# Rotary halves of the queries at rows 0 and 64: the turned copy read from the other rows, not multiplied, and a new order table for the middle

## The chip, the cores and the metric

The kernel runs on one core of one Trainium2 chip, in one launch. The metric is the device time in microseconds; before the change three runs gave 1440.78, 1445.82 and 1445.23 us, a median of 1445.23.

## What is computed

One layer of a hybrid trunk for 1056 tokens: 1024 of a new prompt and 32 of a running stream with 512 cached positions. Three mixers (latent attention with 6 heads, an S5 state-space model, RWKV-7 with 6 heads) read one input projection and meet in one output projection; a layer norm, a squared-ReLU MLP and a second layer norm follow. The change touches the attention's queries:

```python
cos, sin = rope_tables(pos)
q = (rms_norm(q_lat, prm['q_norm_g']) @ prm['w_qb']).reshape(b, t, MLA_HEADS, NOPE_DIM + ROPE_DIM)
q_nope = q[..., :NOPE_DIM]
q_rope = apply_rope(q[..., NOPE_DIM:], cos, sin)
...
x1, x2 = jnp.split(xf, 2, axis=-1)
return (xf * c + jnp.concatenate([-x2, x1], -1) * s).astype(x.dtype)
```

Each head has 64 columns without rotation (nope) and 32 with it (rope). A rotated row is the row times a cosine, plus the row of the other half of the 32 (the turned copy) times a sine whose sign depends on the half.

## The kernel before

The work stands in this order: the input projection to about 241 us of the profiled execution, then stage_q (241 to 262), the middle (262 to about 676) in which attention, S5 and RWKV are interleaved, the output projection with the first layer norm, and the MLP from some 780 us on. The program is written as stages; a scheduler with a timeline model of its own then sets the order of instructions on each engine, within what the code ties down. Tokens lie along the free axis, 1056 columns, cut in three blocks of 384, 384 and 288.

**stage_q** (L1175 to L1228) turns the normalized query latent qn (256 x 1056) into the queries. Its function product (L1184 to L1192) makes 128 rows of output: for each of the three blocks two matmuls with a weight of 128 columns (k is the half of the 256), named scq, and an eviction by ScalarE. Six products are made: qrope (the 32 rotary rows of heads 0 to 3), qturn (the same rows with their halves exchanged, multiplied from a second copy of the weight whose columns are exchanged), qropeb (for heads 4 and 5 rows and turned rows together, 64 and 64), and three qnope, two heads each (L1202). wqa and wqr are the weights: wqr is loaded with 8 DMAs on ScalarE's queue (L1199), wqa with two on SP's. ropec and ropes hold cosines and signed sines, repeated per head (four loads each, L1210 on SP's queue, L1211 on ScalarE's). VectorE does the rotation with six operations: L1215 to L1217 on 128 rows for heads 0 to 3, and L1222 to L1224 on 64 rows for heads 4 and 5, where L1222 reads qropeb's rows 64 to 127 and writes rows 0 to 63. The results go to q_d in DRAM: four stores of 32 rows (L1220) and two qnope stores on SP's queue, the rest on GpSimd's. attn_q (L1231) reads a head's 96 rows back.

**Behind stage_q on SP's queue** stand loads of the cached keys (ct, kt; the rows in which the new rotary keys kr arrive, L1107, are cleared around by two VectorE memsets, L1115 and L1116), the first head's q, the stores zt_d and xt_d of RWKV operands (zt is a VectorE copy, L778, after a loop of L774 and L775), and the loads zb and zc of them (L791, L792), which the pti matmuls (L802) of the RWKV inversion read. Of the kr rows ScalarE makes the rounded kh, VectorE the remainder kl (split3, L49 and L50); the attention's score matmuls sc and st (three each, L63, L65, L67) need both.

**The middle** (L1363) pulls one step at a time from four streams, as the letters of the string PLAN say: F is the front of a head's attention (sc, and the maximum mx on VectorE), O its back (st, the exponential ptk on ScalarE, the product with the values av, L1289), S is the RWKV scan (names that begin with pr, such as pra, prt, prw, and pti), X is S5 (s5e L643, s5y, s5l). Each step is tied behind the TensorE instruction of the step before it, so PLAN sets TensorE's order to a large part. S5 reads em by SP's queue (L632); after its last block it stores z_d, reads it back turned as zt (8 DMAs on SP's queue and 8 on GpSimd's, L690), and applies a gelu on ScalarE (L697) with a table load before and behind it. An out-projection (acc<-wo,m) starts in the middle's last part as filler; its last input is mg_d, the store of the last head's ot, which comes back as mraw and is split to mh and ml. z is the first layer norm (L1540 to L1543), which TensorE turns (pt, L1562).

Of the kernel before, what the change touches and what calls it, by code (L numbers as in the profile page):

```python
# [8 lines left out]
F32 = mybir.dt.float32  # L9
F32R = mybir.dt.float32r  # L10
AF = mybir.ActivationFunctionType
ALU = mybir.AluOpType
# [5 lines left out]
P = 128  # L18
T = 1056
# [707 lines left out]
def hsl(i):  # L727
    return slice(64 * i, 64 * i + 64)
# [446 lines left out]
def stage_q(g):  # L1175


    nc = g.nc
    i = 0

    def f(name):
        return g.p1.tile([P, T], F32, tag="f", name=name, bufs=5)

    def product(out, w):  # L1184
        nonlocal i
        for s, n in BLK:
            pool, tag = ((g.pfs, "fs"), (g.pt, "pt"))[i % 2]
            i += 1
            ps = pool.tile([P, 512], F32, tag=tag, name="scq")[:, :n]
            for k in range(2):  # L1190
                nc.tensor.matmul(out=ps, lhsT=w[:, k], rhs=g.qn[:, k, s:s + n], start=k == 0, stop=k == 1)  # L1191
            nc.scalar.activation(out=out[:, s:s + n], in_=ps, func=AF.Copy)  # L1192

    wa = f("wqa")[:, :768].rearrange("p (k h c) -> p k h c", k=2, c=64)
    wr = f("wqr")[:, :768].rearrange("p (k j x) -> p k j x", k=2, x=P)
    for k in range(2):
        nc.sync.dma_start(out=wa[:, k], in_=g.a["w_qb"][:, k, :, 0:64])
        for h, n, c, j, x in ((0, 4, 64, 0, 0), (0, 4, 96, 1, 0), (4, 2, 64, 2, 0), (4, 2, 96, 2, 64)):
            nc.scalar.dma_start(out=wr[:, k, j, x:x + 32 * n].rearrange("p (h c) -> p h c", c=32), in_=g.a["w_qb"][:, k, h:h + n, c:c + 32])  # L1199
    qs_ = g.xp.tile([P, KD, T], F32, tag="xl", name="qnope")  # L1200

    def nope(p):  # L1202
        q = qs_[:, KD - 3 + p]
        product(q, wa[:, :, 2 * p:2 * p + 2].rearrange("p k h c -> p k (h c)"))
        for h in range(2):
            (nc.gpsimd if p else nc.sync).dma_start(out=g.q_d[2 * p + h, 0:64], in_=q[hsl(h)])

    cs, sn = f("ropec"), f("ropes")
    for h in range(4):
        nc.sync.dma_start(out=cs[32 * h:32 * h + 32], in_=g.a["rope"][0:32])  # L1210
        nc.scalar.dma_start(out=sn[32 * h:32 * h + 32], in_=g.a["rope"][32:64])  # L1211
    qa, qs, qb, qt = (g.p1.tile([P, 1152], F32, tag="kk", name=x, bufs=3)[:, :T] for x in ("qrope", "qturn", "qropeb", "qturnb"))
    product(qa, wr[:, :, 0])
    product(qs, wr[:, :, 1])
    nc.vector.tensor_tensor(out=qa, in0=qa, in1=cs, op=ALU.mult)  # L1215
    nc.vector.tensor_tensor(out=qs, in0=qs, in1=sn, op=ALU.mult)
    nc.vector.tensor_tensor(out=qa, in0=qa, in1=qs, op=ALU.add)  # L1217
    nope(0)
    for h in range(4):
        nc.sync.dma_start(out=g.q_d[h, 64:96], in_=qa[32 * h:32 * h + 32])  # L1220
    product(qb, wr[:, :, 2])
    nc.vector.tensor_tensor(out=qt[0:64], in0=qb[64:128], in1=sn[64:128], op=ALU.mult)  # L1222
    nc.vector.tensor_tensor(out=qb[0:64], in0=qb[0:64], in1=cs[0:64], op=ALU.mult)
    nc.vector.tensor_tensor(out=qb[0:64], in0=qb[0:64], in1=qt[0:64], op=ALU.add)  # L1224
    nope(1)
    nope(2)
    for h in range(2):
        nc.gpsimd.dma_start(out=g.q_d[4 + h, 64:96], in_=qb[32 * h:32 * h + 32])  # L1228


def attn_q(g, h):  # L1231
# [131 lines left out]
def middle(g, scan):  # L1363
# [36 lines left out]


PLAN = (
    "FFFFFFFFSFSFFSFFFFFFSFFFFFFFFFFFSFOOSOFSOOOSFOOOSSOSOOSFSOFOFOOOOOOSXOSOOFSFOSXOOOOFOOOSFFSSSOSSOOXF"
    "FXFOSFOFOSOSXFFFOOFSOSSOSXOOSFSFSOOFSOFXXOSOFOFOOOOSOFSSOFOXOOXFSOOOFOFOOSOXSSSOOSOFSOFXSFSFOOFFSSFX"
    "FFFSFFFSXOOSFOOSOFOOSOOXFSSOOSXFOSOOSOOSFXOOOOFOOXOSFSSOOFSSOXOSOOOOOFOSXOFFSOXSFSFFSFFSFFSOOXSOSFFX"
    "SSFOOSOOOXOSOOOFSOOOOOFSOFOOSOOXSOFSSOXOFOOSFXXFOXOSSOOFSOSFXOOOOSSFOFSXFFFSFFFFSFFFSXFFFSFFSOXOOSSO"
    "OFSOXOSFFOSOSOXOFSOOFSOXFOSOSXOSFOOOSOOOOOFSSOSXSFOOOOSFOXFOXOSOSFOFOSSSFFSFFOOSSOOOOOOOOOOSOOOOSOFS"
    "SOSSOOOOSSOSOOOOOOOOOOOOOO"
)


# [803 lines left out]
def tile_trunk(ctx, tc, a, o):  # L2215
# [31 lines left out]
    with ExitStack() as s1:  # L2247
# [47 lines left out]
        nc.sync.dma_start(out=g.o["sh_s"], in_=sho[10:20])  # L2295
        stage_u(g)
        stage_q(g)
        s2.close()
    g.pt = None
# [144 lines left out]
```

## Time and profile before

| | us |
|---|---|
| median of three runs (lowest, highest) | 1445.23 (1440.78, 1445.82) |
| the profiled execution's own time | 1446.23 |
| its span, first to last instruction | 1444.5 |
| TensorE busy in the span | 1378.9 |
| mean granted TensorE clock, of full speed | 0.976 |
| stage_q's 72 scq matmul records | 241.0 to 262.2 |

A line of the timeline gives start, duration, engine, line, operation, out<-in, shapes, a count, and in brackets how long the engine had been idle and what ended that. A wait row gives the waiting engine and line, what released it, then the sum in us, the number of times and the longest. A row of the windows gives for a stretch its length, the busy time of each engine with the number of instructions, the granted clock (1.00 is full), the DMA share and GB/s. In a row of one tile, three numbers with strokes are the shortest, median and longest duration in ns. An fp32 matmul shows as two records.

### The profile page before, as it was taken

To read this page: it belongs to the slowest core of one execution; us is meant where nothing else is said; L and a number is where in the kernel's file an instruction comes from. 1 tells how busy PE (TensorE), PEld (TensorE's weight loads), DVE (VectorE), ACT (ScalarE), POOL (GpSimd) and SP (SyncE) were. 2 spreads that over 40 slices of the span, in tenths; PEclk is the share of its full clock that TensorE was granted. 3 is DMA by queue.
4 is the path that set the end of the run, shared out by engine and by line. 5 is a ranking of instruction groups with operands and counts; after the bars stand their busy time and mean duration, and the time that the engine had idled before them with its cause. 6 is when DMAs were issued, how large, how long until landed. Compare 5 with 4: busy or idle time off the path is not lost.

```text
span 1444.5 us, 28201 instructions
## 1 busy us (share of the span) xinstructions
PE 1378.9 (95%) x11532; PEld 1238.2 (86%) x11532; DVE 981.1 (68%) x1793; ACT 656.6 (45%) x1143; POOL 114.9 (8%) x228
## 2 busy tenths in 40 slices
PE   9999999789999879899998999999999999999996
PEld 9989898576777657667688999999999999999996
DVE  7666979655666755664769876666655786665577
ACT  6645543435454545552326344444444443434332
POOL 1411100400000100200200000000000000000022
PEclk9999999799999999899999999999999999999998
DMA  5433553941343420244434444344429695354232
GB/s 204 148 124 136 173 158 92 235 84 51 92 108 89 97 55 27 80 128 135 121 106 152 156 166 150 122 161 147 145 107 392 226 323 164 96 180 129 64 103 77
DMA packets 149431, 198.59 MB, mean 137 GB/s; under 512 B 53393, under 2 KB 97093, under 8 KB 148793
## 3 DMA queue, kind: packets, MB, share of 16 engines
q1 hardware_dynamic: 128492, 176.19, 38.5%
q10 hardware_dynamic: 20072, 18.50, 4.2%
q0 software_dynamic: 736, 2.09, 0.6%
q8 instruction: 90, 1.47, 0.4%
q14 instruction: 41, 0.33, 0.1%
HBM read 129.42 MB, written 67.28 MB: 136 GB/s over the span
## 4 chain that ended last, share of the span: by engine, by line
PE 81%; DVE 9%; ACT 4%; DMA 2%; issue 2%; SPq 1%; POOL 0%; ACTq 0%; DVEq 0%; POOLq 0%
PE acc L63 20%; PE acc L67 20%; PE acc L65 20%; PE av L1289 3%; PE scq L1191 1%; DMA wo<-in_w_out 1%; DVE mx L1260 1%; PE st L63 1%; PE sc L63 1%; PE st L65 1%; PE st L67 1%; PE scv L1169 1%; PE prw L896 1%; DVE xo L50 1%; PE pti L802 1%
## 5 line engine op out<-in xcount | busy, mean ns | idle before, releaser
L63 PE MATMUL acc<-xo,wo 128*128 128x272 f32 (+1 forms) x896 | 254.7, 285 | 2.8 <-ACT wo L49 2.8
L67 PE MATMUL acc<-xo,wo 128*128 128x256 f32 (+1 forms) x896 | 253.6, 285 | 1.6 <-DVE wo L50 1.6
L65 PE MATMUL acc<-xo,wo 128*128 128x272 f32 (+1 forms) x896 | 253.7, 284 | 0.0
L67 PE MATMUL acc<-hop,wo 128*128 128x272 f32 (+1 forms) x896 | 194.4, 284 | 0.0
L63 PEld LDWEIGHTS acc<-xo,wo 128*128 128x128 f32 x896 | 168.8, 189 | 3.0 <-ACT wo L49 3.0
L67 PEld LDWEIGHTS acc<-xo,wo 128*128 128x128 f32 x896 | 168.4, 189 | 2.0 <-DVE wo L50 2.0
L65 PEld LDWEIGHTS acc<-xo,wo 128*128 128x128 f32 x896 | 169.3, 189 | 0.0
L63 PE MATMUL acc<-hop,wo 128*128 128x256 f32 (+1 forms) x768 | 159.1, 285 | 0.0
L65 PE MATMUL acc<-hop,wo 128*128 128x272 f32 (+1 forms) x768 | 158.3, 283 | 0.0
L67 PEld LDWEIGHTS acc<-hop,wo 128*128 128x128 f32 x896 | 142.4, 188 | 0.0
L63 PE MATMUL acc<-xh,wmhi 128*128 128x384 f32 (+3 forms) x384 | 127.2, 332 | 2.1 <-ACT ckv L204 1.8
L65 PE MATMUL acc<-xl,wmhi 128*128 128x384 f32 (+3 forms) x384 | 128.1, 334 | 0.7 <-DVE xl L50 0.6
L67 PE MATMUL acc<-xh,wmlo 128*128 128x384 f32 (+3 forms) x384 | 127.1, 332 | 0.0
L65 PEld LDWEIGHTS acc<-hop,wo 128*128 128x128 f32 x768 | 119.6, 189 | 0.0
L63 PEld LDWEIGHTS acc<-hop,wo 128*128 128x128 f32 x768 | 118.7, 188 | 0.0
L49 ACT ACTIVATE wo<-wr 128x512 fp32r<-128x512 f32 (+1 forms) x64 | 47.0, 739 | 117.9 <-PE acc L67 68.0
L1289 PE MATMUL av<-ptk,vo 128*128 128x512 f32 (+5 forms) x204 | 74.5, 450 | 10.3 <-ACT ptk L1314 9.0
L50 DVE TENSOR_TENSOR hop<-hraw,hop 128x1056 fp32r<-128x1056 f32 (+3 forms) x58 | 70.4, 1214 | 13.8 <-ACT hop L49 13.7
L50 DVE TENSOR_TENSOR wo<-wr,wo 128x512 fp32r<-128x512 f32 (+1 forms) x64 | 52.3, 822 | 40.3 <-ACT wo L49 40.3
L63 PEld LDWEIGHTS acc<-xh,wmhi 128*128 128x128 f32 (+1 forms) x384 | 71.7, 187 | 5.2 <-ACT ckv L204 1.9
L65 PEld LDWEIGHTS acc<-xl,wmhi 128*128 128x128 f32 (+1 forms) x384 | 71.6, 187 | 4.4 <-DVE xl L50 1.3
L67 PEld LDWEIGHTS acc<-xh,wmlo 128*128 128x128 f32 (+1 forms) x384 | 71.7, 187 | 3.5 <-issue 1.6
(558 smaller groups left out, 2973.2 us busy)
## 6 DMA issues: line engine op xcount, KB each, us to landing
hraw<-h_d SPq DMA_DIRECT2D x48, 528.0 KB
wr<-in_w_up SPq DMA_DIRECT2D x35, 512.0 KB
h_d<-hx SPq DMA_DIRECT2D x16, 792.0 KB
h_d<-ht SPq DMA_DIRECT2D x16, 792.0 KB
wd<-in_w_dn SPq DMA_DIRECT2D x16, 512.0 KB
wr<-in_w_dn SPq DMA_DIRECT2D x16, 512.0 KB
ld<-rw SPq DMA_DIRECT2D x24, 320.0 KB
wmraw<-in_w_m SPq DMA_DIRECT2D x12, 512.0 KB
```

What stands on the lines that cost most here:

```text
L49: nc.scalar.activation(out=hi, in_=ps, func=AF.Copy)
L50: (lo_eng or nc.vector).tensor_tensor(out=lo, in0=ps, in1=hi.bitcast(F32), op=ALU.subtract)
L63: nc.tensor.matmul(out=outs[i], lhsT=lh, rhs=rhs[i][0], start=start, stop=False, **kw)
L65: nc.tensor.matmul(out=outs[i], lhsT=lh, rhs=rhs[i][1], start=False, stop=False, **kw)
L67: nc.tensor.matmul(out=outs[i], lhsT=ll, rhs=rhs[i][0], start=False, stop=stop, **kw)
L802: nc.tensor.matmul(out=ps[64 * c:64 * c + 32, t], lhsT=l[rows, t], rhs=z[rows, t], start=True, stop=True)
L896: nc.tensor.matmul(out=pw[hsl(c), p - p0, h], lhsT=g.xt[p][hsl(c), t, h], rhs=r[hsl(c), p, K_A:K_NV + 1:K_NV, h], start=True, stop=True)
L1169: nc.tensor.matmul(out=ps[:n, j], lhsT=c, rhs=g.wkv[:, 1, p * P:p * P + P], start=True, stop=True)
L1191: nc.tensor.matmul(out=ps, lhsT=w[:, k], rhs=g.qn[:, k, s:s + n], start=k == 0, stop=k == 1)
L1260: nc.vector.tensor_reduce(out=mx[:n, t, b // 512:b // 512 + 1], in_=ps[:n, :w], axis=AX.X, op=ALU.max)
L1289: nc.tensor.matmul(out=po[:, c:n], lhsT=vo[:w, kt].rearrange("p a x -> p (a x)")[:, 64 * i:64 * i + P], rhs=pt[:w, c:n], start=kt == tiles ...
```

## The change

The rotary columns of the weight are laid out anew: first halves (16 rows of each head) from row 0, second halves from row 64. Then the turned copy of a row is the row 64 further on, or back, and qturn's product goes; wr shrinks from three groups to two. Heads 4 and 5 take 96 rows: 0 to 31 first halves, 32 to 63 a filler (the first halves again), 64 to 95 second halves. product takes outputs of fewer than 128 rows.

VectorE's rotation becomes nine operations. For heads 0 to 3: two products on 64 rows that read one half of q and write the other half of a temporary (qropet), one product with the cosine and one sum on 128 rows. For heads 4 and 5: two products on 32 rows, one on 96, two sums on 32. A half of a head is 16 rows, so the loads and stores are cut finer: wqr 10 loads instead of 8 (ScalarE's queue), ropes 8 loads of 16 rows on SP's queue instead of 4 of 32 on ScalarE's, qrope 8 stores of 16 rows on SP's queue instead of 4, qropeb 4 on GpSimd's instead of 2. The rotation is a generator (turn), whose stores are issued after nope(0).

```diff
-                nc.tensor.matmul(out=ps, lhsT=w[:, k], rhs=g.qn[:, k, s:s + n], start=k == 0, stop=k == 1)
-            nc.scalar.activation(out=out[:, s:s + n], in_=ps, func=AF.Copy)
+                nc.tensor.matmul(out=ps[:out.shape[0]], lhsT=w[:, k], rhs=g.qn[:, k, s:s + n], start=k == 0, stop=k == 1)
+            nc.scalar.activation(out=out[:, s:s + n], in_=ps[:out.shape[0]], func=AF.Copy)
...
-        for h, n, c, j, x in ((0, 4, 64, 0, 0), (0, 4, 96, 1, 0), (4, 2, 64, 2, 0), (4, 2, 96, 2, 64)):
-            nc.scalar.dma_start(out=wr[:, k, j, x:x + 32 * n].rearrange("p (h c) -> p h c", c=32), in_=g.a["w_qb"][:, k, h:h + n, c:c + 32])
+        for h, n, c, j, x in ((0, 4, 64, 0, 0), (0, 4, 80, 0, 64), (4, 2, 64, 1, 0), (4, 2, 64, 1, 32), (4, 2, 80, 1, 64)):
+            nc.scalar.dma_start(out=wr[:, k, j, x:x + 16 * n].rearrange("p (h c) -> p h c", c=16), in_=g.a["w_qb"][:, k, h:h + n, c:c + 16])
...
-        nc.scalar.dma_start(out=sn[32 * h:32 * h + 32], in_=g.a["rope"][32:64])
-    qa, qs, qb, qt = (g.p1.tile([P, 1152], F32, tag="kk", name=x, bufs=3)[:, :T] for x in ("qrope", "qturn", "qropeb", "qturnb"))
-    product(qa, wr[:, :, 0])
-    product(qs, wr[:, :, 1])
-    nc.vector.tensor_tensor(out=qa, in0=qa, in1=cs, op=ALU.mult)
-    nc.vector.tensor_tensor(out=qs, in0=qs, in1=sn, op=ALU.mult)
-    nc.vector.tensor_tensor(out=qa, in0=qa, in1=qs, op=ALU.add)
+        for a in range(2):
+            nc.sync.dma_start(out=sn[64 * a + 16 * h:64 * a + 16 * h + 16], in_=g.a["rope"][48 - 16 * a:64 - 16 * a])
+
+    def turn(name, m, w, heads):
+
+        q, t = (g.p1.tile([P, 1152], F32, tag="kk", name=x, bufs=3)[:, :T] for x in (name, name + "t"))
+        product(q[0:m], w)
+        r = m - 64
+        for a in range(2):
+            nc.vector.tensor_tensor(out=t[64 * a:64 * a + r], in0=q[64 - 64 * a:64 - 64 * a + r], in1=sn[64 - 64 * a:64 - 64 * a + r], op=ALU.mult)
+        nc.vector.tensor_tensor(out=q[0:m], in0=q[0:m], in1=cs[0:m], op=ALU.mult)
+        for x in ((slice(0, P),) if r == 64 else (slice(0, r), slice(64, m))):
+            nc.vector.tensor_tensor(out=q[x], in0=q[x], in1=t[x], op=ALU.add)
+        yield
+        for j, h in enumerate(heads):
+            for a in range(2):
+                (nc.sync if h < 4 else nc.gpsimd).dma_start(out=g.q_d[h, 64 + 16 * a:80 + 16 * a], in_=q[64 * a + 16 * j:64 * a + 16 * j + 16])
+
+    ta, tb = turn("qrope", P, wr[:, :, 0], range(4)), turn("qropeb", 96, wr[:, :, 1, 0:96], (4, 5))
+    next(ta)
     nope(0)
-    for h in range(4):
-        nc.sync.dma_start(out=g.q_d[h, 64:96], in_=qa[32 * h:32 * h + 32])
...
+    next(ta, None)
+    next(tb)
     nope(1)
     nope(2)
-    for h in range(2):
-        nc.gpsimd.dma_start(out=g.q_d[4 + h, 64:96], in_=qb[32 * h:32 * h + 32])
+    next(tb, None)
```

PLAN gets a new string of the same kind; its first line as an example:

```diff
-    "FFFFFFFFSFSFFSFFFFFFSFFFFFFFFFFFSFOOSOFSOOOSFOOOSSOSOOSFSOFOFOOOOOOSXOSOOFSFOSXOOOOFOOOSFFSSSOSSOOXF"
+    "FFFFFFFFSFSFFFFFFFSFSFFFFFFFFFFFSFOOSOFSOOOSFOOOSSOSOOSFSOFOFOOOOOOOOSSXOFSOFSXOFOOOFOOOSFSSSOSSOOXF"
```

What this makes of the order, in three places. First SP's queue behind stage_q, before and then after (q_d holds the queries, ct, kt and kr are keys):

```order
L1220 DMA q_d<-qrope 32x1056 x2
L1206 DMA q_d<-qnope 64x1056 x2
L1220 DMA q_d<-qrope 32x1056 x2
L1088 DMA ct<-in_ckv 128x4x128
L1094 DMA kt<-in_kr 128x4x32
L1107 DMA kr<-kr_d 32x1056
```

And after:

```order
L1206 DMA q_d<-qnope 64x1056 x2
L1227 DMA q_d<-qrope 16x1056 x8
L1088 DMA ct<-in_ckv 128x4x128
L1094 DMA kt<-in_kr 128x4x32
L1107 DMA kr<-kr_d 32x1056
```

The qnope stores stand first, and eight short qrope stores in place of four stand between them and the key loads. The rest of the queue (q, zt_d, xt_d, zb, zc) keeps its order.

Second, TensorE at the first s5e of S5, in the middle's first quarter; the piece of the difference, lines with a minus are of before:

```order
-L896 MATMUL prw<-r,xt 64x128 x12
-L643 MATMUL s5e<-ut,em 128x133 x2
-L1289 MATMUL av<-ptk,vo 128x32
-L847 MATMUL pra<-ld 64x128 x12
+L1297 MATMUL av<-ptk,vo 128x32
 L63 MATMUL st<-qh,kh 128x512
 L65 MATMUL st<-ql,kh 128x512
 L67 MATMUL st<-qh,kl 128x512
-L1289 MATMUL av<-ptk,vo 128x32
+L896 MATMUL prw<-r,xt 64x128 x12
+L847 MATMUL pra<-ld 64x128 x12
+L643 MATMUL s5e<-ut,em 128x133 x2
```

s5e moved behind one group of st (128x512) and behind pra.

Third, TensorE at the S5 output, where av waits for an exponential that ScalarE makes after the gelu; before, with the waiting av as the last row:

```order
L847 MATMUL pra<-ld 64x128 x12
L63 MATMUL st<-qh,kh 128x512
L65 MATMUL st<-ql,kh 128x512
L67 MATMUL st<-qh,kl 128x512
L1132 MATMUL sck<-ckv,wkv 128x32
L854 MATMUL prt<-ident,ld 128x128 x8
L1289 MATMUL av<-ptk,vo 128x512
L63 MATMUL st<-qh,kh 128x512
L65 MATMUL st<-ql,kh 128x512
L67 MATMUL st<-qh,kl 128x512
L1289 MATMUL av<-ptk,vo 128x512
```

And after, again up to the av whose exponential follows the gelu on ScalarE:

```order
L1297 MATMUL av<-ptk,vo 128x512
L847 MATMUL pra<-ld 64x128 x12
L63 MATMUL st<-qh,kh 128x512
L65 MATMUL st<-ql,kh 128x512
L67 MATMUL st<-qh,kl 128x512
L854 MATMUL prt<-ident,ld 128x128 x8
L1297 MATMUL av<-ptk,vo 128x512
L63 MATMUL st<-qh,kh 128x512
L65 MATMUL st<-ql,kh 128x512
L67 MATMUL st<-qh,kl 128x512
L854 MATMUL prt<-ident,ld 128x128 x4
L1297 MATMUL av<-ptk,vo 128x512
```

Ahead of these rows one more group of st (128x512) stands since the change, and one exponential more is made before the gelu; so one st, one av and four prt more lie between the loads of zt and the waiting av. Elsewhere in the middle steps are exchanged in many places; the last av of the middle has 86 and not 105 of the output projection's matmuls ahead of it. Outside stage_q the TensorE instructions are the same ones.

More of the change, by code (lines that the diff above doesn't have):

```diff
@@ L1190, in product @@
             for k in range(2):
-                nc.tensor.matmul(out=ps, lhsT=w[:, k], rhs=g.qn[:, k, s:s + n], start=k == 0, stop=k == 1)
-            nc.scalar.activation(out=out[:, s:s + n], in_=ps, func=AF.Copy)
+                nc.tensor.matmul(out=ps[:out.shape[0]], lhsT=w[:, k], rhs=g.qn[:, k, s:s + n], start=k == 0, stop=k == 1)
+            nc.scalar.activation(out=out[:, s:s + n], in_=ps[:out.shape[0]], func=AF.Copy)
     wa = f("wqa")[:, :768].rearrange("p (k h c) -> p k h c", k=2, c=64)
-    wr = f("wqr")[:, :768].rearrange("p (k j x) -> p k j x", k=2, x=P)
+    wr = f("wqr")[:, :512].rearrange("p (k j x) -> p k j x", k=2, x=P)
     for k in range(2):
         nc.sync.dma_start(out=wa[:, k], in_=g.a["w_qb"][:, k, :, 0:64])
-        for h, n, c, j, x in ((0, 4, 64, 0, 0), (0, 4, 96, 1, 0), (4, 2, 64, 2, 0), (4, 2, 96, 2, 64)):
-            nc.scalar.dma_start(out=wr[:, k, j, x:x + 32 * n].rearrange("p (h c) -> p h c", c=32), in_=g.a["w_qb"][:, k, h:h + n, c:c + 32])
+        for h, n, c, j, x in ((0, 4, 64, 0, 0), (0, 4, 80, 0, 64), (4, 2, 64, 1, 0), (4, 2, 64, 1, 32), (4, 2, 80, 1, 64)):
+            nc.scalar.dma_start(out=wr[:, k, j, x:x + 16 * n].rearrange("p (h c) -> p h c", c=16), in_=g.a["w_qb"][:, k, h:h + n, c:c + 16])
     qs_ = g.xp.tile([P, KD, T], F32, tag="xl", name="qnope")
@@ L1210, in stage_q @@
         nc.sync.dma_start(out=cs[32 * h:32 * h + 32], in_=g.a["rope"][0:32])
-        nc.scalar.dma_start(out=sn[32 * h:32 * h + 32], in_=g.a["rope"][32:64])
-    qa, qs, qb, qt = (g.p1.tile([P, 1152], F32, tag="kk", name=x, bufs=3)[:, :T] for x in ("qrope", "qturn", "qropeb", "qturnb"))
-    product(qa, wr[:, :, 0])
-    product(qs, wr[:, :, 1])
-    nc.vector.tensor_tensor(out=qa, in0=qa, in1=cs, op=ALU.mult)
-    nc.vector.tensor_tensor(out=qs, in0=qs, in1=sn, op=ALU.mult)
-    nc.vector.tensor_tensor(out=qa, in0=qa, in1=qs, op=ALU.add)
-    nope(0)
-    for h in range(4):
[L1220 to L1224, printed above, removed]
+        for a in range(2):
[15 more added lines that the diff above has]
+    next(ta)
+    nope(0)
+    next(ta, None)
+    next(tb)
     nope(1)
     nope(2)
-    for h in range(2):
-        nc.gpsimd.dma_start(out=g.q_d[4 + h, 64:96], in_=qb[32 * h:32 * h + 32])
+    next(tb, None)
 def attn_q(g, h):
@@ L1402 @@
 PLAN = (
-    "FFFFFFFFSFSFFSFFFFFFSFFFFFFFFFFFSFOOSOFSOOOSFOOOSSOSOOSFSOFOFOOOOOOSXOSOOFSFOSXOOOOFOOOSFFSSSOSSOOXF"
[L1404 to L1408, printed above, removed]
+    "FFFFFFFFSFSFFFFFFFSFSFFFFFFFFFFFSFOOSOFSOOOSFOOOSSOSOOSFSOFOFOOOOOOOOSSXOFSOFSXOFOOOFOOOSFSSSOSSOOXF"
+    "FXFOSFOFOSOSXFFFFOOSOSSOSOXOSFSFOSFSOOFXOXOSFOFOOOOSOFFSSOXOFOOXOOSOFOFOOOXSOOSSSOFSSOFXSFSFOOFFSSFX"
+    "FFFSFFFSOXOSFOOSOFOOXFSOOSSSXOOFSSOOOOSOFXOOOOFOOXOSFSSOOOFSSOXOSOOOOFOSXOFFFFSOXFFSFSSFFSSOOXSOSFFO"
+    "XSSFOSOOOXOSOOOFSOOOOOFSOFOOOOOSXFOSOSSXFOOFXSXFXOOOSOSFOSSFXOOOOSSFOXFSFFFSFFFFSFFFFSXFFSFFSOXOOSSO"
+    "FSOXOSFFOOSOSOFXOSOOFSOXFOSOSXOSFOOOSOOOOOFXSSOSSFOOOFOSOXFOXOSOSFOFOSSSFSFFFOSSOOOOOOOOOOSOOOOOSOFO"
+    "SOSOOOSSOSSOOOOOSOOOOOOOOO"
 )
```

## The prediction

> **What bounds the kernel now.** I read the page first, for shares and for the chain that ended last.
>
> ```profile
> PE 1378.9 (95%) x11532; PEld 1238.2 (86%) x11532; DVE 981.1 (68%) x1793; ACT 656.6 (45%) x1143; POOL 114.9 (8%) x228
> PE 81%; DVE 9%; ACT 4%; DMA 2%; issue 2%; SPq 1%; POOL 0%; ACTq 0%; DVEq 0%; POOLq 0%
> ```
>
> TensorE is busy for 1378.9 of 1444.5 us and is 81% of the chain. So the change can gain in two ways only: fewer TensorE instructions where TensorE is itself the limit, or shorter waits among the 65.6 us in which it stands still. Next came TensorE's waits by line, and the busy time stretch by stretch.
>
> ```profile
> PE av L1289 <- ACT ptk L1314: 9.0, 2, 8.0
> PE sc L63 <- DVE kl L50: 4.9, 1, 4.9
> PE s5e L643 <- DMA em<-em_d: 2.3, 1, 2.3
> ...
> core 0: us, PE busy (x) PEld busy (x) DVE busy (x) ACT busy (x) POOL busy (x), PEclk, DMA share, GB/s
> 241.00:262.20 21.20, 21.20 (x75) 13.63 (x74) 15.94 (x24) 8.36 (x18) 1.72 (x4) 1.00 0.55 142
> 262.20:300.00 37.80, 27.15 (x403) 19.72 (x401) 24.65 (x52) 14.91 (x25) 14.25 (x18) 0.77 0.76 175
> 500.00:540.00 40.00, 28.98 (x297) 19.81 (x296) 19.04 (x50) 16.63 (x27) 1.39 (x5) 0.91 0.26 63
> ```
>
> During stage_q, 241 to 262, TensorE never stops. Straight after it, 10.65 us of 37.8 are idle and the granted clock is 0.77: the start of the middle waits for other engines. That is the place to which anything saved in stage_q is handed. The chain of waits there, in order of time:
>
> ```profile
> 241.29 21.31 PE scq L1191 x72
> ...
> 263.06 1.08 ACT qh L1124
> 264.14 0.97 ACT ql L1124
> 265.14 1.17 ACT kh L49 x2
> ...
> 275.72 0.47 PE sc L63
> 276.63 1.87 PE pti L802 x64
> ```
>
> From 263.06 on the chain is ScalarE and VectorE, until the first sc matmul at 275.72, which waited the 4.9 us of the second waits row.
>
> **The removed product.** Six products are the 72 matmul records of 21.31 us, so one is 3.55 us, and 384 of its 1056 columns are 1.29 us. Removing qturn frees TensorE and the last qnope eviction 3.55 us earlier. ScalarE could then reach kh at 261.6 and not at 265.14. What is late next decides how much of this arrives: kh reads kr, whose rows VectorE clears after the turn, and kr is loaded by SP behind the qrope stores.
>
> **VectorE.** Its rows in stage_q, from the timeline:
>
> ```profile
> 246.61 1.26 DVE L1215 TENSOR_TENSOR qrope<-qrope,ropec 128x1056 f32<-128x1056 f32 x1 [1.17 <-ACT qrope L1192]
> ...
> 252.00 1.05 DVE L778 COPY zt<-y 108x1024 f32<-108x1024 f32 x1
> ...
> 256.05 1.25 DVE L1222 TENSOR_TENSOR qturnb<-qropeb,ropes 64x1056 f32<-64x1056 f32 x1 [3.00 <-ACT qropeb L1192]
> 258.62 1.25 DVE L1224 TENSOR_TENSOR qropeb<-qropeb,qturnb 64x1056 f32<-64x1056 f32 x1
> 261.37 0.94 DVE L1116 MEMSET kr<- 1x1056 f32 x1 [0.28 <-DMA kr<-kr_d]
> ```
>
> A turn operation takes 1.26 us on 128 rows and 1.25 on 64, so the rows don't set its time, and I price those on 32 and 96 rows at 1.25 too. Nine in place of six add 3.8 us. The first four start where the three started, since one 384-column part of another product stands ahead of qrope's last part as before (now of qnope, then of qturn). Between 246.61 and 253.05 there were 6.44 us of work: 3.77 of turn and 2.67 of other. With four it is 7.7, to 254.3. By then qropeb is there, and the 3.00 us wait before L1222 is gone; that idle time hides most of the rest. Five operations end at 260.6, against 259.87. Two clears of 0.94 us with 0.28 between follow, to 263.0: VectorE alone would leave 2.1 of the 3.55 us.
>
> **SP.** Its rows, first one load on ScalarE's queue:
>
> ```profile
> 238.15 0.90 ACTq L1199 DMA_DIRECT2D wqr<-in_w_qb  x2
> ...
> 251.56 0.78 SPq L1220 DMA_DIRECT2D q_d<-qrope  x2
> ...
> 255.63 0.43 SPq L1088 DMA_DIRECT2D ct<-in_ckv  x1
> 256.76 0.61 SPq L1107 DMA_DIRECT2D kr<-kr_d  x1
> ...
> 270.95 2.03 SPq L792 DMA_DIRECT2D zb<-xt_d  x4
> ...
> L1220 SPq DMA_DIRECT2D q_d<-qrope x4: 309/560/1219, 251.6 to 254.4; - x4
> ```
>
> The two qnope stores now stand ahead of the qrope stores, in SP's long wait, and cost nothing. The rotary result comes after four operations and 0.95 us of other work, at 252.6 rather than 251.5. Then eight stores in place of four: at the least of that row, 0.31 each, they take 2.5 us; at the greatest, 1.22, they take 9.8. I take the median, 0.56, thus 4.5, because these are short issues in a run. ct moves to 257.1, 1.5 us later, and kr, q, zt_d, xt_d and the zb loads with it. kr was issued at 256.76 and let the last clear start at 261.37, 4.6 us on; now that is 262.9, the clear ends at 263.8, and kh starts 1.3 us earlier than before. The first pti reads zb: two of the four loads of 270.95, some 0.5 us apart, issued now by 273.0. A comparable load is em below, issued at 316.28 and used at 320.00, 3.7 us. So zb is there at about 276.7, where the pti started at 276.6 before. Sc gains 1.3 us, pti nothing; I take 0.5 us for the front, between a gain of 3.55 and a loss of 7.
>
> [...]
>
> The other moves are covered. The cosine and sine loads go to SP at 225, long before use at 246. The second half of the second wqr block, which the first product reads, slips to the place of the row at 238.15; by em's 3.7 us it is there at 242.3. Four matmuls of 0.65 us (wqr and wqa of the first block) now precede its use, at 243.9.
>
> **The table, at the em wait.** Timeline of TensorE with SP's load of em:
>
> ```profile
> 316.28 0.50 SPq L632 DMA_DIRECT2D em<-em_d  x1
> ...
> 320.00 0.69 PE L643 MATMUL s5e<-ut,em 128*128 128x133 f32 x4 [2.30 <-DMA em<-em_d]
> ...
> 320.77 1.15 PE L847 MATMUL pra<-ld 64*64 64x128 f32 x24
> 321.85 0.50 PE L63 MATMUL st<-qh,kh 128*128 128x512 f32 x1
> ...
> 322.74 0.40 PE L1289 MATMUL av<-ptk,vo 32*128 32x32 f32 x2
> ```
>
> pra (320.77 to 321.85) and st (321.85 to 322.74) now stand ahead of s5e and fill 1.97 of its 2.30 us. The em load hangs on SP and not on this work, so I count -2.0; if pra or st find their own inputs late it is 0.
>
> **The table, at the gelu.** The wait of 8.0 us is ScalarE's: it holds a gelu that waits for loads of zt, and the exponentials behind it.
>
> ```profile
> 493.62 4.23 POOL L690 DMA_DIRECT2D zt<-z_d  x8 [5.91 <-PE av L1289]
> ...
> 499.24 1.07 PE L854 MATMUL prt<-ident,ld 128*128 128x128 f32 x8
> 500.15 1.02 PE L1289 MATMUL av<-ptk,vo 128*128 128x512 f32 x2
> 500.61 0.80 PE L63 MATMUL st<-qh,kh 128*128 128x512 f32 x1
> 509.86 2.08 PE L1289 MATMUL av<-ptk,vo 128*128 128x512 f32 x2 [8.00 <-ACT ptk L1314]
> ```
>
> The loads start from the same av as before, and between that av and the one that waits there is now one st more (0.89, as at 321.85), one av (0.46, from 500.15 to 500.61) and half of the prt (0.53): 1.9 us of the 8.0. I count -1.8, between 0 and -1.9.
>
> In that stretch the clock was 0.91. [...]
>
> **The table, at the end of the middle.**
>
> ```profile
> 673.84 0.63 PE L63 MATMUL acc<-wo,mh 128*128 128x512 f32 x2
> 674.31 0.62 PE L65 MATMUL acc<-wo,mh 128*128 128x512 f32 x2
> ...
> 681.42 0.65 PE L63 MATMUL acc<-wo,mh 128*32 128x512 f32 x2 [0.47 <-ACT mh L49]
> 684.29 1.97 PE L1562 MATMUL pt<-ident,z 128*128 128x128 f32 x8 [1.75 <-DVE z L1543]
> 686.91 1.06 PE L67 MATMUL acc<-wo,ml 128*32 128x512 f32 x2 [0.65 <-DVE ml L50]
> ```
>
> The last av now comes with 86 and not 105 of the output projection's matmuls ahead of it: 19 of 0.235 us, 4.4 us earlier, and the softmax's rest, the store of the head and the first normalization move with it. The three waits hold 2.9 us. I count half, -1.5, since the same matmuls then come behind.
>
> **Against it.** With fewer fillers between them the last st and av wait for exponentials, and an order that is re-dealt in many places opens waits that no row of before shows. The bounds are -1.0 (the second av wait in the row of 9.0, two, 8.0 may close as well) and twice the em wait, +4.6; I take +1.5, nearer to the small ones.
>
> The sum is -0.5 - 2.0 - 1.8 - 1.5 + 1.5 = -4.3 us. The profiled execution took 1446.23 us, 1.0 more than the median of the three runs, so a like one after the change takes 1441.9, and the median 1445.23 becomes 1440.9. A measurement of this kernel can tell about 0.5%, 7.2 us: faster means below 1438.0, slower above 1452.5.
>
> **Rivals.** (a) As summed: 1440.9, chance 0.45. (b) All of it arrives: the short stores issue at 0.31 us, ct is not late, VectorE leaves 2.1 us at the front, em -2.0, gelu -1.8, the end -2.9 and no new waits: -8.8, thus 1436.4; a front that idles less may regain some of the clock of 0.77 as well, which reaches to about 1432. For it speaks the minimum of the stores' row, against it its median; 0.27. (c) The table only trades waits, and the front's 0.5 remains: 1444.7; 0.14. (d) Slower: SP becomes the bound at the front. Each store at 1.22 us puts ct at 262.4, 6.8 later, and zb and the first pti as much; TensorE, at a clock of 0.77 in this stretch, idles that much more, and 8 us of its 27.15 at half clock instead of full are another 4: 1445.2 + 6.8 + 4 - 3.8 for the table = 1452.2, and 1456 if the table's own new waits eat its gain. It decides from about 1.0 us per store. For it speaks the row's greatest value, against it that only one of the four was so slow; 0.10. [...] (e) The change doesn't do what it says: reading the other half's rows doubles the four shifted operations. VectorE and the stores end 2.5 us later, pti with them, at +2.5; with the table -3.8 that is 1443.9. L1222 reads other rows already and takes 1.25, so 0.04.
>
> **The numbers.** Faster: nearly all of (b) and a fifth of (a), 0.34. Slower: (d) and a little of (c), 0.12. Same: the rest, 0.54. The range takes in (b) with its clock, (a), (c) and (e): 1432 to 1450; what is left out is most of (d) and an odd tail. The likeliest case's own range is 1437 to 1445.
>
> **What would show it.** Right: six DVE operations become nine of about 1.25 us; ct issues near 257; the first sc starts near 274.4 and the first pti near 276.7; the wait at s5e is under 0.5, at the gelu near 6.1, and those at the end sum to under 1.5. Wrong: ct before 255.6 or after 260; shifted operations over 1.5 us; the em or gelu wait unchanged; new waits over 3 us in the middle, where none stood.

## The result, and the profile after

The changed kernel takes 1435.31 us (median of seven runs, 1433.35 to 1441.88); the kernel before took 1445.82 in seven runs beside it. The ratio is 0.9939, with an interval of 0.9912 to 0.9966: 0.6% faster, 8.8 us (the ratio goes by the means; the medians differ by 10.5). The profiled execution took 1435.31 us, its span is 1433.5.

First the busy times of the page, then TensorE's waits by line (total, times, longest):

```profile
PE 1367.7 (95%) x11520; PEld 1230.7 (86%) x11520; DVE 989.9 (69%) x1796; ACT 654.4 (46%) x1140; POOL 113.3 (8%) x230
```

```profile
PE av L1297 <- ACT ptk L1322: 9.7, 6, 6.0
...
PE sc L63 <- DVE kl L50: 5.4, 1, 5.4
...
PE sc L63 <- DVE sc L1267: 3.2, 1, 3.2
...
PE s5e L643 <- DMA em<-em_d: 0.6, 1, 0.6
```

TensorE is busy 11.2 us less (1378.9 before). The wait at em is nearly gone and the one at the gelu is down from 8.0 to 6.0. The wait of the first sc for kl is still there, and a second sc now waits 3.2 us. To see where the 11.0 us between the two spans went, I cut both at the same instructions. The times are starts in the two timelines.

| boundary | before | after | the stretch before it changes by |
|---|---|---|---|
| first scq | 241.13 | 238.11 | -3.02 |
| first scm (end of the front) | 294.86 | 292.82 | +0.98 |
| second group of s5e (behind em) | 325.80 | 322.18 | -1.58 |
| s5l | 496.91 | 492.19 | -1.10 |
| seventh prk (behind the gelu) | 515.88 | 509.66 | -1.50 |
| last prw | 620.02 | 614.00 | +0.20 |
| second pt of z | 701.78 | 689.74 | -6.02 |
| end of the span | 1444.5 | 1433.5 | +1.04 |

**Ahead of stage_q** the TensorE instructions stand in the same order in both kernels. The windows near 90 us differ, first before, then after:

```profile
89.60:93.00 3.40, 3.40 (x12) 3.06 (x11) 3.40 (x5) 1.04 (x3) 0.00 (x0) 0.61 0.00 0
93.00:96.40 3.40, 3.40 (x16) 2.73 (x16) 2.38 (x17) 0.91 (x2) 0.00 (x0) 0.89 0.58 238
```

```profile
89.60:93.00 3.40, 3.40 (x19) 3.07 (x19) 3.37 (x8) 0.89 (x3) 0.00 (x0) 1.00 0.00 0
93.00:96.40 3.40, 3.40 (x19) 2.48 (x18) 1.97 (x15) 2.25 (x5) 0.00 (x0) 1.00 0.72 290
```

TensorE never stops in these rows, yet in the kernel before the clock is at about half for some 3.4 us (0.61 and 0.89 in its two rows, 1.00 in those of after). Another half-clock stretch of 3.4 us, near 171, stands in this profile of the kernel before and not in that of after; it is in five of the twelve profiles here (0.91 over 165 to 185), whatever the kernel. I come back to this under what stays open.

**The front.** The chain of waits of after, then rows of the timeline (start, duration, engine, line):

```profile
254.10 6.22 DMA kr<-kr_d
260.40 1.17 ACT kh L49 x2
...
268.74 5.46 DMA q<-q_d
274.22 0.64 ACT qh L49
```

```profile
249.43 3.56 SPq L1227 DMA_DIRECT2D q_d<-qrope  x8
253.04 0.42 SPq L1088 DMA_DIRECT2D ct<-in_ckv  x1
...
262.87 5.76 SPq L791 DMA_DIRECT2D zb<-zt_d  x4
268.74 2.06 SPq L1244 DMA_DIRECT2D q<-q_d  x1
...
270.99 0.47 PE L63 MATMUL sc<-kh,qh 128*128 128x128 f32 x1 [5.36 <-DVE kl L50]
...
271.82 1.92 PE L802 MATMUL pti<-zb,n 32*32 32x32 f32 x64
276.96 0.55 PE L63 MATMUL sc<-kh,qh 128*128 128x256 f32 x1 [3.22 <-DVE sc L1267]
```

Counted from the first scq, the first sc comes 1.71 us earlier than before (32.88 after it, 34.59 before). Then TensorE waits 3.22 us for the second head's q, which SP loads behind four loads of zb, and these wait for their store. So scm comes 0.98 later, though TensorE has 3.55 us less to do on the way: its idle time between the first scq and scm grows from 10.65 to 15.47 us, so all of the removed product became idle time.

**The end of the middle.** The same place as in the prediction's last rows, now of after, then windows (length, busy times, the granted clock third from the end) of before and of after:

```profile
675.93 0.63 PE L63 MATMUL acc<-wo,mh 128*32 128x512 f32 x2
...
676.85 1.03 PE L1570 MATMUL pt<-ident,z 128*128 128x128 f32 x8
677.64 0.70 PE L67 MATMUL acc<-wo,ml 128*32 128x512 f32 x2
```

```profile
680.80:684.20 3.40, 1.27 (x5) 0.35 (x4) 3.37 (x7) 1.38 (x6) 0.00 (x0) 1.00 1.00 360
684.20:687.60 3.40, 2.66 (x10) 1.92 (x11) 3.40 (x10) 2.16 (x5) 0.00 (x0) 0.51 0.21 59
687.60:691.10 3.50, 3.50 (x9) 1.37 (x8) 3.50 (x7) 2.51 (x8) 2.49 (x2) 0.50 0.71 187
691.10:694.50 3.40, 3.40 (x16) 1.62 (x15) 3.40 (x8) 0.49 (x3) 1.47 (x1) 1.00 0.52 154
```

```profile
680.00:700.00 20.00, 20.00 (x96) 13.83 (x95) 19.43 (x28) 8.88 (x25) 10.62 (x6) 1.00 0.53 151
```

All three waits are gone, 2.87 us. Before, the window with the first two of them was busy for 1.27 of 3.40 us, and the next two windows ran at a granted clock of 0.51 and 0.50, with 2.66 + 3.50 = 6.16 us of work. The eight pt records took 1.97 us there and take 1.03 in after, so I estimate that this work takes half as long at full clock, and that 3.1 us more were lost. 2.87 + 3.1 is 6.0, the -6.02 of the table.

### The profile page after: what moved, and what is told of

The parts are those of the page before. It is cut to its first block, busy times and chain, and to the rows that moved or that the text cites. A ratio compares the mean times of both kernels' runs of the same rounds, so it can differ in the third digit from the quotient of the medians.

```text
span 1433.5 us, 28198 instructions
## 1 busy us (share of the span) xinstructions
PE 1367.7 (95%) x11520; PEld 1230.7 (86%) x11520; DVE 989.9 (69%) x1796; ACT 654.4 (46%) x1140; POOL 113.3 (8%) x230
## 4 chain that ended last, share of the span: by engine, by line
PE 77%; DVE 10%; DMA 5%; ACT 4%; issue 2%; SPq 2%; POOL 0%; ACTq 0%; DVEq 0%; POOLq 0%
PE acc L63 20%; PE acc L65 20%; PE acc L67 20%; PE av L1297 3%; DMA wo<-in_w_out 1%; DVE mx L1268 1%; PE sc L63 1%; DVE wo L50 1%; PE st L63 1%; PE scv L1169 1%; PE prw L896 1%; PE st L65 1%; PE st L67 1%; PE sc L65 1%; PE sc L67 1%
## 5 line engine op out<-in xcount | busy, mean ns | idle before, releaser
L1297 PE MATMUL av<-ptk,vo 128*128 128x512 f32 (+5 forms) x204 | 74.2, 447 | 10.5 <-ACT ptk L1322 9.7
L49 ACT ACTIVATE hop<-hraw 128x1056 fp32r<-128x1056 f32 (+3 forms) x58 | 60.6, 1045 | 30.2 <-PE acc L67 29.1
L49 ACT ACTIVATE wo<-ws 128x512 fp32r<-128x512 f32 x64 | 39.9, 628 | 75.6 <-PE acc L67 66.3
```

Of the source, the lines that this page charges most:

```text
L49: nc.scalar.activation(out=hi, in_=ps, func=AF.Copy)
L1297: nc.tensor.matmul(out=po[:, c:n], lhsT=vo[:w, kt].rearrange("p a x -> p (a x)")[:, 64 * i:64 * i + P], rhs=pt[:w, c:n], start=kt == tiles ...
```

## The experiments

The theory was: the gain is the table's, in three places (em, gelu, the end), and the end pays twice, in waits and in clock; the removed product buys only idle time. The rivals were: the new stage_q gains by its shorter work; the gain is spread over many exchanged steps; the clock has nothing to do with it. All ratios are to the kernel before, on the same chip.

**Only the new stage_q** (the old PLAN), and **only the new PLAN** (the old stage_q); of each edit one line, against after:

```diff
 # newq_oldtab (and the five lines of PLAN behind it)
-    "FFFFFFFFSFSFFFFFFFSFSFFFFFFFFFFFSFOOSOFSOOOSFOOOSSOSOOSFSOFOFOOOOOOOOSSXOFSOFSXOFOOOFOOOSFSSSOSSOOXF"
+    "FFFFFFFFSFSFFSFFFFFFSFFFFFFFFFFFSFOOSOFSOOOSFOOOSSOSOOSFSOFOFOOOOOOSXOSOOFSFOSXOOOOFOOOSFFSSSOSSOOXF"
...
 # oldq_newtab (and the rest of stage_q)
-    wr = f("wqr")[:, :512].rearrange("p (k j x) -> p k j x", k=2, x=P)
+    wr = f("wqr")[:, :768].rearrange("p (k j x) -> p k j x", k=2, x=P)
...
```

> The new stage_q with the old order table. Theory: the removed product brings TensorE to the first key matmuls some 3 us earlier, but the load of the second head's q and the zb loads give it back within 40 us, and the gain of 8 to 9 us is the table's: within 2 us of before (ratio 0.9985 to 1.0015), and counted from the first scq matmul the first scm comes 0 to 1.5 us later than before. Rival one, the product is the gain: ratio 0.994. Rival two, the front keeps its 3.2 us: ratio 0.998 and the first scm 3 us earlier.

> The old stage_q, all six products, with the new table. Theory: the table is the gain, so 8 to 10 us below before, ratio 0.993 to 0.9945; the end of the middle without waits and at full clock. Rival (the product is the gain): within 2 us of before.

Measured: 0.9999 (0.9980 to 1.0018) for the new stage_q alone, 0.9927 (0.9901 to 0.9953) for the table alone. The table is the whole gain, and the product's 21 us to 18 us on TensorE is worth nothing that can be measured. From the first scq to the first scm the distances say the same: 53.73 before, 53.56 with the new stage_q, 53.45 with the new table, 54.71 with both. One profile is a weak witness here: two more kernels below have the new stage_q, the old table and the same TensorE order up to this point, and they give 53.83 and 57.20. With the table alone, the end runs without a stop, as in after:

```profile
680.00:700.00 20.00, 20.00 (x97) 13.76 (x95) 19.50 (x28) 8.95 (x25) 10.66 (x6) 1.00 0.52 153
```

**The end exchanged: first cut.** The last 53 letters of PLAN, from the 474th on, were exchanged, once back in after and once forward in the new stage_q with the old table (the last line is shown, the letters ahead of it go with it):

```diff
 # newtab_oldend, against after
-    "SOSOOOSSOSSOOOOOSOOOOOOOOO"
+    "SOSSOOOOSSOSOOOOOOOOOOOOOO"
 # oldtab_newend: the same, the other way round, against newq_oldtab
```

> The whole change, but the last 53 letters of the table are the old ones, so 105 matmuls of the output projection stand ahead of the last av again. Theory (the end is worth 5 us, 2.9 of waits and some 2 of a clock that they halve): ratio to before 0.997 to 0.999, the clock of the stretch at the last av again near 0.83, the waits at mh, z and ml back. Rival (only the waits count, the rest of the gain lies in the middle): ratio 0.995 to 0.9965.

> The new stage_q with the old table, but its last 53 letters are the new ones. Theory: 4 to 5 us below before, ratio 0.9965 to 0.9975, no waits and clock 1.00 at the end of the middle. Rival (the end alone is worth the 1.5 to 2.9 us of its waits): ratio 0.998 to 0.999.

Measured: 0.9999 (0.9981 to 1.0016) and 0.9989 (0.9972 to 1.0007). Both are further toward 1 than I expected, because the cut was not clean. Each opened a wait that neither parent has. The timeline row of newtab_oldend, then that of oldtab_newend with two of its windows:

```profile
609.25 0.72 PE L954 MATMUL pry<-gq,st 64*64 64x64 f32 x12 [2.99 <-DVE st L961]
```

```profile
634.11 2.08 PE L1297 MATMUL av<-ptk,vo 128*128 128x512 f32 x2 [4.54 <-ACT po L1302]
```

```profile
620.00:640.00 20.00, 14.92 (x164) 10.23 (x163) 14.44 (x26) 10.44 (x19) 1.57 (x1) 0.83 0.59 175
...
680.00:700.00 20.00, 20.00 (x99) 12.81 (x98) 19.96 (x35) 9.84 (x25) 6.17 (x3) 1.00 0.52 152
```

In the second kernel the end is mended (680 to 700 at full clock), and the new wait of 4.54 us, with a clock of 0.83 around it, takes the gain back; that is read from the trace.

**The end exchanged: second cut.** Only the last 18 letters, behind which the last av has 105 or 86 matmuls of the output projection ahead of it:

```diff
 # newtab_oldend508, against after
-    "SOSOOOSSOSSOOOOOSOOOOOOOOO"
+    "SOSOOOSSSSOSOOOOOOOOOOOOOO"
 # oldtab_newend508, against newq_oldtab
-    "SOSSOOOOSSOSOOOOOOOOOOOOOO"
+    "SOSSOOOOOSSOOOOOSOOOOOOOOO"
```

> The changed kernel with only the last 18 letters of the old table. Theory (the end is worth 5 us: 2.9 us of waits at mh, z and ml and some 2 of a clock that falls to half for 6 us): ratio to before 0.997 to 0.998, those waits back, pt of z with 8 records again near 2 us instead of 1. Rival (what the run with the last 53 old letters lost came from letters before these 18): ratio 0.994 to 0.9955.

> The new stage_q with the old table, of which only the last 18 letters are new. Theory (the end alone is worth 6 to 7 us, as taking it away from the new table cost): ratio to before 0.995 to 0.997, no waits at mh, z and ml and clock 1.00 there. Rival (the end pays only behind the rest of the new table; alone its wait moves to an av that waits for its PSUM, as with the 53 letters): ratio 0.998 to 1.0, a wait of 3 us or more near 634 us.

Measured: 0.9986 (0.9968 to 1.0004) with the old end put back, 0.9955 (0.9937 to 0.9974) with the new end alone. Against 0.9939 and 0.9999 that is 0.47% and 0.44%, 6.8 and 6.4 us, by two kernels whose tables otherwise differ; by the intervals each is good to some 0.3%, 4 us or more. All twelve profiles agree: the wait of 1.74 to 1.75 us at pt and a half-clock stretch behind it (0.83 to 0.91 over 680 to 700) stand in all four with the old end and nothing in it, and in none of the seven with the new end (1.00). The windows of the old end put back show the loss of clock again, those of the new end alone don't:

```profile
679.80:683.30 3.50, 1.71 (x7) 0.51 (x5) 3.46 (x6) 1.62 (x7) 0.00 (x0) 1.00 0.92 337
683.30:686.70 3.40, 2.50 (x10) 1.84 (x11) 3.40 (x10) 1.99 (x4) 0.00 (x0) 0.50 0.33 94
686.70:690.10 3.40, 3.40 (x10) 1.35 (x9) 3.40 (x7) 2.68 (x9) 2.22 (x2) 0.50 0.69 183
```

```profile
680.00:700.00 20.00, 20.00 (x99) 12.82 (x98) 19.93 (x36) 9.56 (x28) 5.19 (x2) 1.00 0.54 161
```

**The old end with its idle time filled.** If idle time costs clock, useless work in it should keep the clock. Four matmuls, whose result is overwritten, were put ahead of the first pt of z:

```diff
 # oldend_filled, against newtab_oldend508
+        if i == 0 and h == 0:
+            for _ in range(NDUM):
+                nc.tensor.matmul(out=pt.rearrange("p k c -> p (k c)"), lhsT=g.ident, rhs=g.gb[:, 0, 0:512], start=True, stop=True)
...
+NDUM = 4
```

> The changed kernel with the last 18 letters of the old table (as newtab_oldend508), and four matmuls of 0.47 us whose result is never used (their PSUM is overwritten) ahead of the last head's first output-projection matmul, where TensorE stood still. They add 1.9 us of work and no product of use. Theory (the short waits there cost more by the clock they halve than by themselves): the granted clock stays 1.00 over that stretch, pt of z takes about 1 us instead of 2, and the time is 2 to 4 us below newtab_oldend508, ratio to before 0.9955 to 0.9975. Rival (the clock doesn't depend on these waits, or the idle time alone counts): as newtab_oldend508 or up to 1.9 us above it, ratio 0.9985 to 1.0.

Measured: 0.9966 (0.9951 to 0.9981), as forecast, but the interval overlaps that of the unfilled kernel. Its timeline, and one window:

```profile
679.28 3.60 PE L1570 MATMUL pt<-gb,ident 128*128 128x512 f32 x8
...
683.63 1.03 PE L1573 MATMUL pt<-ident,z 128*128 128x128 f32 x8
685.22 0.66 PE L67 MATMUL acc<-wo,ml 128*32 128x512 f32 x2 [0.55 <-DVE ml L50]
```

```profile
680.00:700.00 20.00, 19.45 (x88) 11.03 (x87) 19.93 (x39) 7.71 (x20) 4.67 (x2) 1.00 0.49 145
```

The half-clock windows are gone, and the same eight pt records take 1.03 us instead of 1.97. So here the loss of clock, 0.50 for 6.8 us without the four matmuls and 1.00 with them, does come from the idle time. But the four matmuls, eight records, took 3.60 us where I had counted 1.9, and from the last full-width acc to the second pt the stretch is as long as without them (678.81 to 698.93, and 679.77 to 699.80: 20.12 and 20.03). The profile shows an even trade; that the filled kernel is the faster one by 0.2% rests on the times alone and is not settled.

**The letters at em put back** (the 68th to 72nd):

```diff
 # newtab_old_em, against after: OOSSX becomes SXOSO
-    "FFFFFFFFSFSFFFFFFFSFSFFFFFFFFFFFSFOOSOFSOOOSFOOOSSOSOOSFSOFOFOOOOOOOOSSXOFSOFSXOFOOOFOOOSFSSSOSSOOXF"
+    "FFFFFFFFSFSFFFFFFFSFSFFFFFFFFFFFSFOOSOFSOOOSFOOOSSOSOOSFSOFOFOOOOOOSXOSOOFSOFSXOFOOOFOOOSFSSSOSSOOXF"
```

> The changed kernel with five letters of the old table, which put s5e back ahead of one st group and pra. Theory: the wait for em is 2.0 to 2.7 us again instead of 0.6, and 1.4 to 2.0 us are lost over the changed kernel, ratio 0.995 to 0.9955. Rival (a later wait absorbs it): the wait is back and the ratio is the changed kernel's.

Measured: 0.9966 (0.9940 to 0.9991), 0.27% or 3.9 us above after, though the intervals overlap. The wait is back, and here it costs more than its length. First the wait and three windows in this kernel, then two windows around the same wait of 2.30 us in the kernel before:

```profile
319.45 0.69 PE L643 MATMUL s5e<-ut,em 128*128 128x133 f32 x4 [2.34 <-DMA em<-em_d]
```

```profile
317.00:320.40 3.40, 1.06 (x12) 0.94 (x12) 0.00 (x0) 0.60 (x2) 0.00 (x0) 1.00 0.93 278
320.40:323.80 3.40, 3.40 (x28) 2.32 (x25) 1.06 (x2) 0.98 (x4) 0.00 (x0) 0.50 0.13 29
323.80:327.20 3.40, 3.40 (x13) 3.05 (x14) 0.93 (x5) 1.69 (x5) 0.00 (x0) 0.50 0.02 4
```

```profile
315.60:319.00 3.40, 2.10 (x32) 1.80 (x31) 2.05 (x3) 1.36 (x6) 0.00 (x0) 1.00 0.92 193
319.00:322.40 3.40, 2.40 (x32) 2.15 (x33) 0.71 (x2) 1.17 (x3) 0.00 (x0) 1.00 0.55 192
```

In the kernel before, the wait lies across the border of two windows, each is busy for 60 to 70%, and the clock stays full. Here it falls into one, which is busy for 1.06 of 3.40 us, and 6.8 us at half clock follow. From the first s5e group to the second it is 5.80 us before and 8.86 here. The letters don't decide which: newq_oldtab and oldtab_newend508 have the old letters and the same TensorE order up to here, and the same distance is 5.80 in the profile of the one and 8.86 in that of the other.

**The second head's q loaded earlier.** If SP's queue holds back the front, a buffer of its own for that q, loaded ahead of zb, should take the 3.2 us wait away:

```diff
 # q1_in_ot, against after; oldq_q1_in_ot, the same line against oldq_newtab
-    q = g.ap.tile([P, T], F32, tag="q", name="q", bufs=1)
+    q = g.ap.tile([P, T], F32, tag="ot" if h == 1 else "q", name="q", bufs=1)
```

> The changed kernel; the second head's q gets memory of its own (that of ot, which is free then), so its load stands ahead of the zb loads on SP's queue and need not wait for the first head's q. Theory (this load holds what the removed product freed): the wait of 3.2 us ahead of the second sc group goes, the first scm comes 2 to 3 us earlier counted from the first scq matmul, and the time is 2 to 3 us below that of the changed kernel, ratio to before 0.9915 to 0.993. Rival (the zb loads or the key splits on ScalarE and VectorE are as late as q): the wait moves to pti or the next sc, the first scm gains under 0.7 us, ratio as the changed kernel's, 0.9935 to 0.9945.

> As the run before, but with the old stage_q with its six products. Theory: the product now counts, since nothing behind it waits for that load: the first scm comes, counted from the first scq matmul, about 2 to 3 us later than in the run before, and the ratio is 0.0015 to 0.002 higher. Rival (the front is bound elsewhere): both equal within 0.001, the first scm within 0.7 us.

Measured: 0.9979 (0.9961 to 0.9997) with the new stage_q, 0.9909 (0.9885 to 0.9934) with the old one. The 3.2 us wait is gone in the first, but its waits show where the time went, and those of the second do not have it:

```profile
PE sc L63 <- DVE kl L50: 8.1, 1, 8.1
...
PE av L1297 <- ACT po L1302: 4.4, 2, 3.9
```

```profile
PE sc L63 <- DVE kl L50: 4.9, 1, 4.9
```

ScalarE and VectorE now take up that q ahead of the last rounded keys, and the first sc waits 8.1 instead of 5.4; from the first scq to scm it is 54.04 against 54.71, and within the 54.02 to 55.34 of the other profiles with the new stage_q and the new table, so nothing was gained there. So my step "the wait is SP's" was too short: behind SP stand ScalarE and VectorE. The total got worse because the scheduler placed the output projection's matmuls anew and an av waits 3.9 us for po, with a half-clock stretch near 634 (the clock over 600 to 650 is 0.83, and 0.90 in after); that this is the whole of the loss is read from the trace and wasn't tried by itself. The other kernel, with the old stage_q, has the lowest ratio of all, but its interval overlaps those of after and of the table alone: it is at least as good, not shown better. The rival that the shorter stage_q counts once the queue is out of its way is not borne out: from the first scq to scm the kernel with the product takes 53.24 us, the one without it 54.04. The times alone would not settle it, since the slower kernel also carries the new wait at av.

## Why the prediction was right or wrong

I forecast 1440.9, between 1432 and 1450, and put faster, below 1438.0, at 0.34 beside same at 0.54. It became 1435.3: inside the range, but on the side that I held less likely, and with about twice the gain that I had summed. It is close to rival (b), 1436.4, and that is luck, since the terms that came are not those of (b). One of my signs of being wrong came true, a new wait of over 3 us (3.22, at the second sc). The early ct, at 253.04 and so ahead of my 255.6, is not another: all of stage_q had started 3.02 us earlier.

- **The removed product, -0.5 for the front:** +0.98 in the profile, and nothing in the times of the new stage_q alone. The reason held, that ScalarE, VectorE and SP set the front. The parts: ct was issued 0.43 later counted from the first scq, not 1.5, since the eight stores took 3.56 us, 0.42 each and not 0.56; kr's load took 6.2 us and not 4.6; the first sc came 1.7 us earlier, near the 1.3 I counted. The wrong part is "sc gains, pti nothing": pti came 1.7 us earlier too, and the second sc, which I had not followed, 1.5 us later. The removed product took the cover from the second q's load.
- **VectorE's nine operations:** right. The two on 32 rows took 2.51 us together, 1.25 each. Rival (e) falls.
- **SP as the bound by short stores, rival (d):** it falls at 0.42 us per store. The trace shows the landing of the first store, 1.9 us after its issue; by then four more had been issued, so these times overlap, and the eight took 3.56 us in all. The 4 us of clock in that rival's sum are my estimate for stores of 1.22 us, and no run shows them: the longest of the eight took 0.425, and the granted clock over 262.2 to 300 was 0.78, against 0.77 before.
- **em, -2.0:** 0.59 us of wait are left and the stretch gained 1.58. Right for these two profiles. By the times the letters are worth some 3.9 us, with intervals that overlap; the same wait can cost clock as well.
- **The gelu, -1.8, with no clock in it:** the wait is 6.00 against 8.00 and the stretch gained 1.50; no run tried it alone. But all profiles agree: the wait is 7.58 to 8.00 us in the four with the old table and 4.65 to 6.00 in the eight with the new one. The clock stayed as it was, in before and in after:

```profile
495.00:515.00 20.00, 12.01 (x76) 7.99 (x73) 2.98 (x10) 10.81 (x20) 2.85 (x6) 0.83 0.48 76
```

```profile
495.00:515.00 20.00, 13.92 (x120) 9.32 (x119) 4.51 (x14) 9.75 (x13) 0.29 (x2) 0.83 0.18 40
```

- **The end, -1.5:** this is the step that failed, by its size. I counted half of the waits because the same matmuls come behind. They do, but all of the waiting went, 2.87 us, and with it 3.1 us of half clock that I had not looked for. It was in my own rows: two acc records of the same size took 0.65 us at 681.42 and 1.06 at 686.91, and the eight pt records 1.97, where they take 1.03 after. The second cut confirms it with 6.8 and 6.4 us.
- **New waits, +1.5:** they came, and not only the 3.22 at the second q, which is counted in the front. Before and after, the waits of scm:

```profile
PE scm L1267 <- DVE m L1265: 5.3, 3, 3.3
```

```profile
PE scm L1275 <- DVE m L1273: 6.5, 3, 4.5
```

The longest of them is 3.08 to 3.28 us in the four profiles with the old table and 4.46 to 4.48 in all eight with the new one. The longest wait of acc for wo, near 783 in after, is 2.83 in the four and 4.25 to 4.27 in seven of the eight. Together these two are +2.7. Beyond them a stretch of 3.4 to 6.8 us at half clock, which begins between 524 and 536 (524.5 to 531.3 in after), stands in all eight and in none of the four. The +0.20 from the gelu to the last prw shows little of it because the profile of before was itself slow there: to the last record of prw it took 105.4 us, the other three with the old table 103.0 to 104.6. In the two kernels of the first cut the newly dealt steps cost 2.99 and 4.54 us more. So the fear was sound.

In sum this pair of profiles gives -8.0 apart from the stretch ahead of stage_q, against my -4.3. Of the 3.7 between them the end makes -4.5 and the stretches outside the three places -1.4 (-1.10 + 0.20 + 1.04, together +0.1 in place of +1.5); the front gives back 1.5, em and gelu 0.7. The -1.4 is not a saving of the table. The -1.10 of it is scatter: between the second s5e group and s5l the kernel before ran 6.8 us at half clock near 374 (0.92 over 340 to 380, 1.00 in after), as every other profile did for 3.4 or 6.8 us, and the profile of after alone did not.

**What stays open.** The 3.0 us ahead of stage_q are more than the change does there. About 1.0 of them is the half-clock stretch near 171, which before has and after has not: among the nine profiles with the new stage_q the first scq starts at 237.75 to 238.74 in the six without that stretch and at 239.15 to 239.19 in the three with it. The other stretch, 3.4 us and so worth 1.7 at most, stands in all three profiles of kernels with the old stage_q (near 90 in two, with 0.83 over 90 to 100, and near 79 in oldq_q1_in_ot, with 0.94 over 60 to 90) and in none of the nine with the new one (1.00 in both), with the same TensorE order and no idle time in it or in the window ahead of it. No run separates what makes it, and the times of the new stage_q alone (0.9999, with 0.2% to either side) show no gain from it. The interval of the times, 0.34% to 0.88% or 4.9 to 12.7 us, holds the sum of the parts with it (11.0) and without (8.0), so it doesn't decide either.

## What to carry to other kernels

Price a wait of TensorE by two rows: its own length, and the granted clock of the 6.8 us behind it. A wait of 2 to 3 us cost its length again here, in some executions and not in others: with the old letters at em the same stretch took 8.86 us in one kernel's profile and 5.80 in another's. So read a stretch of a microsecond or two in the profiles of several kernels that share its order, not in one pair. Before counting a removed product, follow not only the first instruction behind it but the next two, and ask for each which queue brings its input. And exchange a piece of an order table both ways, into the one kernel and out of the other: a cut in the wrong place opens waits of its own, and the two answers then disagree.

## What the runs showed of the hardware

**Half clock behind short waits.** Windows of 3.4 us that were busy for 1.06 us (newtab_old_em, from 317.0), 1.27 us (before, from 680.8) and 1.71 us (newtab_oldend508, from 679.8) were each followed by 6.8 us at a granted clock of 0.50 to 0.51; the longest single waits there were 2.34, 1.75 and 1.74 us. Windows busy for 2.10 and 2.40 us (before, from 315.6 and 319.0) were not. The busy time alone doesn't tell them apart: behind windows busy for 1.78 us (newtab_oldend, from 681.2) and 1.93 us (after, from 640.6) the clock stayed full, the eight pt records of the first taking 1.09 us, while one busy for 2.24 of 3.40 us (before, from 370.2) was followed by 6.8 us at half clock, and one without any idle time (before, from 86.9) by 3.4 us. What else decides is open. In the traces of before and after the half-clock stretches, but for the last of each trace, are 3.4 us or a multiple of it long, up to 17.1, and a wait of 2.30 to 2.34 us at em cost clock in one profile and not in another, 8.86 and 5.80 us for the same stretch. And a window at half clock that was busy for 2.50 us (newtab_oldend508, from 683.3) or 2.66 us (before, from 684.2) was followed by another one at half clock.

**Short stores in a row.** Eight stores of 66 KB were issued by SP's queue in 3.56 us, a median of 0.42 each, below the 0.56 of the four stores of twice the size in the kernel before; the first landed 1.9 us after its issue, behind the issue of the fifth.
